# Down projection of a Trainium2 encoder layer: engine order fixed by the source, weight sums by accumulating DMA

## The chip, the cores and the metric

The kernel runs on one core of a Trainium2 chip. The metric is device time in microseconds; several runs are taken and their median counts. One further execution is recorded by the hardware profiler, and its trace is what the profile and the timelines are read from.

The engines go by short names: PE is TensorE (matmuls), DVE VectorE, ACT ScalarE, POOL GpSimd, SP SyncE. Each engine works through its own list of instructions in order; semaphores hold an instruction back until what it needs is there. SP and POOL issue DMAs here.

## The reference, cut to what matters

One encoder layer on a 256 x 2048 input in float32: a half-step feed-forward, a mixer (gated recurrence and windowed attention), and a second half-step feed-forward. The change touches both feed-forwards:

```python
def swiglu(x, w_gate_up, w_down):          # w_gate_up 2048 x 11264, w_down 5632 x 2048
    gate, up = jnp.split(x @ w_gate_up, 2, axis=-1)
    return (jax.nn.silu(gate) * up) @ w_down

ff = swiglu(rms_norm(x, pre_norm_ffn1[layer]), w_ffn1_gate_up[layer], w_ffn1_down[layer])
x = x + 0.5 * rms_norm(ff, post_norm_ffn1[layer])
```

## The kernel before

**Split arithmetic.** Each float32 operand is split in two halves of lower precision: `split_act` (L175 to L177) lets ACT round a block to `h` (L176) and DVE take the remainder `l` (L177). A product of two blocks is then three matmuls: h by h, h by l, l by h (`Blocks.three`, L441). All matmuls of the feed-forwards are of this kind, 128 x 512 wide.

**Pairs.** The contraction runs over pairs of 128 rows. A weight tile `raw` (128 x 2048) holds, for one pair, four blocks of 512 columns: b11, b12 (first 128 rows), b21, b22 (second). A plain pair costs 8 block products, 24 matmuls. A mixed pair uses a scheme of seven block products (21 matmuls) on sums of blocks, on the left (activations, `sums`, split as `sp`) and on the right (weights). On the right it needs the split of b11 (`ha`, `la` in the down projection), then b11+b12 and b22+b12 (one 128 x 1024 addition on DVE, L473), b22 plus the first of these (L477), b21 plus that (L479), and the splits of three halves of the tile, which the text calls lower, upper and last. The seven products ask, in this order, for: the first block; lower; left sums and lower; upper; upper; last; last (`Blocks.products`).

**Feed-forward.** `Gated` forms gate and up in 11 groups of 512 columns, 8 pairs each, 4 of them mixed from the third group on. These groups stand under `tc.manual_schedule()`: each engine has its instructions in the order of the source. There the weight sum b11+b12, b22+b12 of a mixed pair is not formed by DVE: `prepare` (L903) splits the first block, and POOL issues a DMA with `accum_op=add` (L910) that adds the second source block onto the tile in place; `splits` (L917) then goes on with the two dependent additions (L924, L925). After each group `boundary` (L1111) folds the seven-product partial sums (p1, p5, p6, p7) into the four result banks on DVE while PE does the last pair's products bank by bank. The last group is outside: its end is written with `fold()` and left to the scheduler, and so is all of the down projection.

**Down projection.** `Pairs` (L592) goes twice over 22 pairs of activations, once for each half of the 2048 output columns; 10 pairs of each half are mixed (even numbers up to 18), the order of the pairs is in `orders`. `Blocks.work` (L554) loads a tile of 1 MB, splits it and issues the products; a scheduler decides the order on each engine. `seven` (L463) is the mixed pair with the sum on DVE. Weight tiles rotate through three buffers `raw`; the split halves through five `h` and five `l` buffers, so that the last split of a mixed pair behind a mixed pair must wait until PE has released a half of the earlier one. Eight of the activation tiles were put away in DRAM during the gate-up groups and are fetched back into eight buffers (`fetch`, L1039), once. The last two pairs of the second half are held for `finish` (L686), which has its own fixed order.

Of the kernel before, what the change touches and what calls it, by code (L numbers as in the profile page):

```python
# [37 lines left out]
def hymba_layer_kernel(  # L38
# [37 lines left out]
    def nm(s):  # L76
        uid[0] += 1
        return f"{s}_{uid[0]}"
# [323 lines left out]
    class Blocks:  # L402
# [151 lines left out]
        def work(self, upto, among=None):  # L554


            while self.pos < upto:
                u = self.order[self.pos]
                if u in self.mixed:
                    v = self.order[self.pos + 1]  # L560
                    if v not in self.mixed and self.pos + 1 < upto:
                        self.ahead = [v]
                        self.seven(u, self.begin_next)
                    else:
                        self.seven(u)
                else:
                    if self.ahead:
                        _, raw, h, l = self.ahead
                        self.ahead = None
                        hs, ls = zip((h, l), split_half(raw, 1))  # L570
                    else:
                        hs, ls = split_load(self.source(u))
                    if self.pos == self.after + 1 and not self.within:
                        for _ in self.fold():
                            pass
                    places = [(k, m, n) for k in range(2) for m in range(2) for n in range(2)]
                    if self.pos in (self.after, self.after + 1):

                        places.sort(key=lambda at: at[1:])
                    fold = self.fold() if self.within and self.pos == self.after else None  # L580
                    for i, (k, m, n) in enumerate(places):
                        if fold and k == 0:
                            next(fold)
                        if among and i == 3:
                            among()
                        self.plain(u, hs, ls, m, n, k)
                    if fold:
                        for _ in fold:
                            pass
                self.pos += 1  # L590

    class Pairs(Blocks):  # L592

# [21 lines left out]
            self.begin(self.orders[now])  # L615

        def source(self, u):
            src = self.w[u * 2 * P : (u + 1) * 2 * P, self.now * 1024 : (self.now + 1) * 1024]
            return src.rearrange("(k p) c -> p k c", p=P)

        def left_sums(self, u):
            if u in self.kept:
# [54 lines left out]

        def first_run(self):
            self.work(len(self.orders[0]))
            for m in range(2):  # L680
# [177 lines left out]
    class Gated(Blocks):  # L858
# [20 lines left out]
        def plan(self):  # L879

            self.here = {g: MIXED_IN if g > 1 else MIXED_IN[:2] for g in range(1, NG)}
            wanted = []
            for g in range(1, NG):
                for u in range(KT // 2):
                    before = PREPARED[u] if u in self.here[g] else u
                    wanted.append((g * KT // 2 + before, g, u))
            self.wanted = [at[1:] for at in sorted(wanted)]
            self.raws, self.firsts, self.split_of = {}, {}, {}
            for pool, n in ((rawp, 3), (self.room, 2)):
                for _ in range(n):  # L890
                    raw = pool.tile([P, 2048], F32, tag="raw", name=nm("raw"), bufs=n)
                    self.load_next(raw)
# [45 lines left out]
        def take(self, g, u):  # L938
# [2 lines left out]
            del self.raws[g, u]  # L941
            first = self.firsts.pop((g, u), None)
            if first:
                before_fold = g < NG - 1 and u == KT // 2 - 2
# [36 lines left out]
    def ffn(gated, w_dn, post_gain, again, gain=None, lead=None, aside=None):  # L981

        with ExitStack() as st:
# [108 lines left out]
            def some(steps, n):  # L1092
                for _ in range(n):
                    next(steps)
# [13 lines left out]
                    aside()  # L1108
            gated.plan()

            def boundary(g):  # L1111

                a, b = room_for("z"), room_for("s")
                c, (p1, p5, p6, p7) = gated.c, gated.p
# [20 lines left out]
                some(gated.splits(g + 1, 0), 2)  # L1135

            def first_pairs(g, waiting):

# [17 lines left out]
            def pair_ahead(g, u):  # L1156
# [12 lines left out]
                if u == 5 and 1 < g <= AWAY // 2 + 1:  # L1169
                    put_away(2 * g - 4)  # L1170
                    put_away(2 * g - 3)

            waiting = units(gated.c, rs2)
            some(waiting, 2)
            with tc.manual_schedule():
                gated.prepare(1, MIXED_IN[0])
                some(gated.splits(1, 0), 2)
                for g in range(1, NG):
                    first_pairs(g, waiting)
                    for u in range(2, last - 1):  # L1180
                        pair_ahead(g, u)
                    if g < NG - 1:
                        ahead = gated.splits(g, last)
                        some(ahead, 2)
                        gated.prepare(g + 1, MIXED_IN[0])
                        for one in gated.take(g, last - 1):
                            one()
                        boundary(g)
                        waiting = units(gated.c, rest)
                        some(waiting, 2)  # L1190
            some(gated.splits(NG - 1, last), 2)
            gated.take(NG - 1, last - 1)
            a, b = room_for("z"), room_for("s")
            wide = work.tile([P, 2, 512], F32, tag="sp", name=nm("y"), bufs=3)
            gated.folded = lambda: [[a, b], [wide[:, i, :] for i in range(2)]]
            fold = gated.fold()
            final = gated.take(NG - 1, last)
            for m in range(2):
                for n in range(2):
                    next(fold)  # L1200
                    for k in range(2):
                        final[4 * k + 2 * m + n]()
            for _ in fold:
                pass
            waiting = units(gated.c, rest)
            some(waiting, 4)
            room_cm.__exit__(None, None, None)
            close_far()
            back_cm = tc.tile_pool(name=nm("hb"), bufs=AWAY, reuse_waits="tile")
            back = back_cm.__enter__()  # L1210
# [5 lines left out]
            for u in MIXED[8:]:  # L1216
                sums[u] = None
            rows = Pairs(w_dn, orders, hts, sums, work, post_gain, keep=MIXED[8:], near=MIXED[:2])
            rows.half_gain(far["pool"])
# [5 lines left out]
            for u, at in zip(MIXED[8:], (8, 12)):  # L1225
                rows.work(at)
                sums[u] = sums_again(u)
            rows.first_run()
            rows.work(NU - 4)
            back_cm.__exit__(None, None, None)  # L1230
            early_cm.__exit__(None, None, None)
            post = st.enter_context(post_pool())
# [628 lines left out]
```

## Time and profile before

| | |
|---|---|
| median of 3 runs | 1833.16 us (1830.88 to 1833.8) |
| the profiled execution, its own time | 1832.88 us |
| its span, first to last instruction | 1831.1 us |
| mean granted TensorE clock | 0.997 |
| PE busy | 1814.2 us (99%) |
| DVE busy | 1627.3 us (89%) |
| ACT busy | 1129.4 us (62%) |
| POOL busy | 114.4 us (6%) |
| DMA, mean over the span | 231 GB/s |

A row of the windows view gives a stretch in microseconds from the span's start, its length, then for PE, PE's weight loads, DVE, ACT and POOL the busy time with the count of instructions, then the granted clock as a share of full speed, the busy share of the 16 DMA engines, and GB/s. A row of the timeline gives start, duration, engine, line of the kernel, operation, what it writes and reads, and how often it stands there in a row; in square brackets how long the engine had been idle before it and what ended that. Matmuls are pipelined: one shows 0.39 us, but the next starts 0.23 us after it, so starts are compared. A row of groups gives the count, the busy time in us and the mean in ns of one, then the idle time before them.

### The profile page before, as it was taken

The page shows a single profiled execution, that of the slowest core. Times are in us where ns is not written, and L with a number is a line of the kernel's source. Part 1 is how long each engine was busy: PE and PEld are TensorE (multiplying, and loading weights), DVE is VectorE, ACT ScalarE, POOL GpSimd, SP SyncE. Part 2 cuts the span into 40 slices and gives each one's busy share as a digit, 9 for nine tenths or more (in the row PEclk, how much of TensorE's full clock was granted, in tenths as well). Part 3 has the DMA queues.
Part 4 walks back from the last instruction along what each step waited for, and adds up shares of the span by engine and source line. Part 5 has one row for each costly group of instructions (what it writes and reads, how often), then busy time and mean ns, then how long its engine had stood idle before and what let it go on. Part 6 is the DMA issues. An engine that isn't in the chain of part 4 may idle for free.

```text
span 1831.1 us, 23305 instructions
## 1 busy us (share of the span) xinstructions
PE 1814.2 (99%) x8438; PEld 1504.0 (82%) x8438; DVE 1627.3 (89%) x2071; ACT 1129.4 (62%) x1492; POOL 114.4 (6%) x115
## 2 busy tenths in 40 slices
PE   9999999999999999999999999999999999999998
PEld 6888888888887888888888888788888888888886
DVE  7999999999999998477787798899999999999897
ACT  7565666665655666476587556556666666565563
POOL 1011111111000000000000000001111111000000
PEclk9999999999999999999999999999999999999999
DMA  8789999998665566555454456789998998855565
GB/s 301 230 234 283 278 280 253 251 266 241 249 226 197 195 253 216 203 175 178 165 173 150 161 208 249 223 243 267 280 277 267 252 251 251 268 218 207 193 231 185
DMA packets 200020, 422.42 MB, mean 231 GB/s; under 512 B 10984, under 2 KB 45888, under 8 KB 199136
## 3 DMA queue, kind: packets, MB, share of 16 engines
q1 hardware_dynamic: 178880, 380.95, 59.6%
q0 software_dynamic: 21024, 39.99, 12.7%
q8 instruction: 66, 1.08, 0.2%
q14 instruction: 50, 0.41, 0.1%
HBM read 408.29 MB, written 12.60 MB: 230 GB/s over the span
## 4 chain that ended last, share of the span: by engine, by line
PE 87%; DVE 5%; ACT 3%; DMA 3%; issue 2%; POOL 0%; SPq 0%; DVEq 0%; ACTq 0%; POOLq 0%
PE pa L441 37%; PE pb L441 33%; PE pa L309 5%; DVE l L177 3%; PE pa L314 3%; DMA raw<-in_w_ffn_gate_up_dram 2%; PE pa L364 2%; PE pa L362 2%; PE pa L363 2%; ACT h L176 1%; PE pa L1074 1%; PE pb L1074 1%; PE pb L1582 0%; PE pb L1556 0%; PE pb L1660 0%
## 5 line engine op out<-in xcount | busy, mean ns | idle before, releaser
L176 ACT CAST h<-raw 128x1024 fp32r<-128x1024 f32 (+1 forms) x861 | 846.9, 1013 | 448.6 <-PE pb L441 131.9
L177 DVE TENSOR_TENSOR l<-raw,h 128x1024 fp32r<-128x1024 f32 (+1 forms) x861 | 983.1, 1171 | 118.3 <-ACT h L176 83.8
L441 PE MATMUL pa<-h,xt 128*128 128x512 f32 x1104 | 387.2, 392 | 0.1
L441 PE MATMUL pb<-h,xt 128*128 128x512 f32 x952 | 339.7, 391 | 0.4 <-DVE pb L1126 0.4
L441 PEld LDWEIGHTS pa<-h,xt 128*128 128x128 f32 x1104 | 207.2, 188 | 43.9 <-DVE xt L232 0.6
L441 PE MATMUL pa<-l,xt 128*128 128x512 f32 x552 | 215.7, 391 | 0.2 <-DVE l L177 0.2
L441 PEld LDWEIGHTS pb<-h,xt 128*128 128x128 f32 x952 | 178.6, 188 | 43.2 <-DVE pb L1133 3.5
L441 PE MATMUL pb<-l,xt 128*128 128x512 f32 x476 | 185.6, 390 | 0.0
L441 PE MATMUL pb<-h,ht 128*128 128x512 f32 x464 | 163.8, 390 | 0.0
L441 PE MATMUL pa<-h,ht 128*128 128x512 f32 x464 | 163.7, 391 | 0.0
L910 POOL DMA_DIRECT2D raw<-in_w_ffn_gate_up_dram x76 | 92.0, 1211 | 737.0 <-DVE l L177 638.8
L309 PE MATMUL pa<-xt,h 128*128 128x512 f32 x512 | 124.5, 393 | 0.2 <-ACT h L176 0.2
L441 PEld LDWEIGHTS pa<-l,xt 128*128 128x128 f32 x552 | 103.7, 188 | 21.4 <-DVE l L177 1.4
L309 PEld LDWEIGHTS pa<-xt,h 128*128 128x128 f32 x512 | 93.8, 188 | 18.6 <-ACT h L176 0.6
L441 PE MATMUL pa<-h,xs 128*128 128x512 f32 x304 | 108.5, 389 | 0.0
L441 PE MATMUL pb<-h,xs 128*128 128x512 f32 x304 | 105.9, 389 | 0.0
L441 PEld LDWEIGHTS pb<-l,xt 128*128 128x128 f32 x476 | 89.4, 188 | 17.2
L441 PEld LDWEIGHTS pa<-h,ht 128*128 128x128 f32 x464 | 87.7, 189 | 18.4
L441 PEld LDWEIGHTS pb<-h,ht 128*128 128x128 f32 x464 | 87.3, 188 | 18.1
L441 PE MATMUL pa<-l,ht 128*128 128x512 f32 x232 | 90.9, 392 | 0.0
L441 PE MATMUL pb<-l,ht 128*128 128x512 f32 x232 | 90.5, 390 | 0.0
L314 PE MATMUL pa<-xt,l 128*128 128x256 f32 x512 | 69.1, 285 | 0.0
(289 smaller groups left out, 2516.9 us busy)
## 6 DMA issues: line engine op xcount, KB each, us to landing
raw<-in_w_ffn_gate_up_dram SPq DMA_DIRECT2D x350, 512.0 KB, 6.1
raw<-in_w_ffn_down_dram SPq DMA_DIRECT2D x88, 1024.0 KB, 5.3
raw<-in_w_mix_in_dram SPq DMA_DIRECT2D x52, 1024.0 KB, 4.9
raw<-in_w_ffn_gate_up_dram POOLq DMA_DIRECT2D x76, 512.0 KB, 8.8
raw<-in_w_mix_out_dram SPq DMA_DIRECT2D x16, 1024.0 KB, 5.0
away<-ht SPq DMA_DIRECT2D x16, 512.0 KB, 6.9
ht<-away SPq DMA_DIRECT2D x16, 512.0 KB, 7.8
pg<-in_post_norm_ffn_dram SPq DMA_DIRECT2D x4, 512.0 KB, 6.7
```

The source lines that it names most:

```text
L176: nc.scalar.copy(hi, src)
L177: nc.vector.tensor_tensor(lo, src, hi.bitcast(F32), ALU.subtract)
L309: nc.tensor.matmul(slot[f], weights(hs, kk, f), xcol(xt, k), start=(k == 0), stop=(k == KT - 1))
L314: nc.tensor.matmul(slot[f][:, 0:T], weights(ls, kk, f), xcol(xt, kh * 8 + kk, 0), start=False, stop=False,)
L362: nc.tensor.matmul(dst, xh, h[:, o : o + n], start=(k == 0), stop=False)
L363: nc.tensor.matmul(dst, xh, l[:, o : o + n], start=False, stop=False)
L364: nc.tensor.matmul(dst, xl, h[:, o : o + n], start=False, stop=(k == KT - 1))
L441: nc.tensor.matmul(self.bank(at), lhs, rhs, start=(n == 1), stop=n in (ends, self.of[at]), skip_group_check=n > ends,)
L910: nc.gpsimd.dma_start(raw[:, 0:1024].rearrange("p (k c) -> p k c", k=2), self.source(u, g)[:, :, 1], accum_op=ALU.add,)
L1074: nc.tensor.transpose(bank[:, o : o + P], zs[m][:, k * P : (k + 1) * P], ident)
```

## The change

From the last gate-up group to the third last pair of the down projection's second half, everything now stands under the manual schedule, with the order of all engines written in the source:

- The last gate-up group ends with the same `boundary` as the others; the place of the next group's first pair in it is taken by the first pair of the down projection.
- Tiles of the down projection are requested in a list `coming`: when a split has released a tile, `load_down` at once requests the next of the list into it. Five tiles are in use: the three lasting ones, and two in the room of the pool `back`, whose activation buffers go from eight to four; four of the eight activation tiles are therefore fetched a second time (`fetch_at`, steps 26 to 30).
- For 15 of the 20 mixed pairs (`added`: seven in the first half, eight in the second) `prepare` splits the first block three steps ahead, and POOL issues the accumulating DMA in place of DVE's 128 x 1024 sum. Pairs 8, 10 and 18 of the first half and 10 and 18 of the second keep the sum on DVE.
- The left sums of the next mixed pair are split right behind its last weight split (`left_sums_ahead`).
- The orders of the pairs in both halves are new.

The number of matmuls is the same. DVE has 30 instructions fewer (15 in each feed-forward), POOL issues 30 DMAs more, SP 8.

```diff
@@ Gated @@
-                self.rest = 6 if g < NG - 1 else 0
+                self.rest = 6
...
                 self.raws[g, u] = raw
+            elif any(raw is one for one in self.lasting):
+                self.next_stage(raw)
@@ ffn @@
+            orders = [
+                [9, 11, 8, 13, 10, 15, 12, 1, 0, 3, 14, 5, 16, 17, 2, 7, 4, 19, 6, 18, 20, 21],
+                [7, 2, 9, 4, 11, 6, 13, 8, 10, 15, 0, 5, 12, 3, 14, 1, 16, 18, 17, 19, 20, 21],
+            ]
+            added = {0: (12, 0, 14, 16, 2, 4, 6), 1: (2, 4, 6, 8, 0, 12, 14, 16)}
+            in_order = sorted(
+                (i - 2.5 if u in added[r] else i, i) for i, (r, u) in enumerate(steps)
+            )
+            coming = [i for _, i in in_order]
...
+            def prepare(i):
+                if i < len(steps) and steps[i][1] in added[steps[i][0]]:
+                    r, u = steps[i]
+                    first_block(i)
+                    nc.gpsimd.dma_start(
+                        raws[i][:, 0:1024].rearrange("p (k c) -> p k c", k=2),
+                        Pairs.part(w_dn, u, r)[:, :, 512:1024],
+                        accum_op=ALU.add,
+                    )
+
+            def splits(i):
...
+                if i not in firsts:
+                    first_block(i)
+                    nc.vector.tensor_tensor(
+                        four[:, 0:2], four[:, 0::3], four[:, 1:2].to_broadcast([P, 2, 512]), ALU.add
+                    )
+                parts.append(split_half(raw, 1))
+                nc.vector.tensor_tensor(b22, b11, b22, ALU.add)
+                nc.vector.tensor_tensor(b21, b22, b21, ALU.add)
+                yield
+                parts.append(split_half(raw, 0))
+                yield
+                parts.append(split_half(raw, 1))
+                load_down(raw)
+                rows.left_sums_ahead(u)
+                yield
...
-            fold = gated.fold()
-            final = gated.take(NG - 1, last)
-            for m in range(2):
-                for n in range(2):
-                    next(fold)
-                    for k in range(2):
-                        final[4 * k + 2 * m + n]()
-            back_cm = tc.tile_pool(name=nm("hb"), bufs=AWAY, reuse_waits="tile")
-            orders = [
-                [9, 11, 8, 13, 10, 15, 12, 1, 14, 3, 0, 5, 2, 7, 4, 6, 17, 16, 19, 18, 20, 21],
-                [1, 0, 3, 2, 5, 4, 7, 6, 9, 8, 11, 10, 12, 13, 14, 15, 16, 18, 17, 19, 20, 21],
-            ]
-            rows.work(1)
-            rows.work(2, lambda: some(waiting, 2))
-            for i, u in enumerate((1, 3, 0, 5, 2, 7, 4, 6)):
-                fetch(u)
-                rows.work(3 + i // 2)
...
-            rows.first_run()
-            rows.work(NU - 4)
+                    boundary(g, gated.splits(g + 1, 0) if g < NG - 1 else splits(0))
+                    waiting = units(gated.c, rest)
+                    some(waiting, 2)
+                back_cm = tc.tile_pool(name=nm("hb"), bufs=AWAY // 2, reuse_waits="tile")
+                fetch_at = {2: (1, 0), 3: (3,), 5: (5,), 9: (2,), 10: (7,), 11: (4,), 13: (6,)}
+                fetch_at.update({26: (0, 5), 28: (3,), 30: (1,)})
...
+                products(0)
+                for _ in range(2):
+                    load_down(back.tile([P, 2048], F32, tag="raw", name=nm("raw"), bufs=2))
+                some(waiting, 1)
+                ahead = splits(2)
+                some(ahead, 2)
+                some(waiting, 1)
+                some(ahead, 1)
+                products(1)
+                for i in range(2, len(steps)):
...
+                    ahead = splits(i + 1)
+                    next(ahead, None)
+                    prepare(i + 3)
+                    for u in fetch_at.get(i, ()):
+                        fetch(u)
+                    next(ahead, None)
+                    products(i)
+                    for _ in ahead:
+                        pass
```

More of the change, by code (lines that the diff above doesn't have):

```diff
@@ L572, in work, with play @@
                         hs, ls = split_load(self.source(u))
[L573 to L582, printed above, removed]
-                            next(fold)
[L584 to L589, printed above, removed]
-                self.pos += 1
+                    self.play(u, hs, ls, among)
+                self.pos += 1
+        def play(self, u, hs, ls, among=None):
+            if self.pos == self.after + 1 and not self.within:
+                for _ in self.fold():
+                    pass
+            places = [(k, m, n) for k in range(2) for m in range(2) for n in range(2)]
+            if self.pos in (self.after, self.after + 1):
+                places.sort(key=lambda at: at[1:])
+            fold = self.fold() if self.within and self.pos == self.after else None
+            for i, (k, m, n) in enumerate(places):
+                if fold and k == 0:
+                    next(fold)
+                if among and i == 3:
+                    among()
+                self.plain(u, hs, ls, m, n, k)
+            if fold:
+                for _ in fold:
+                    pass
     class Pairs(Blocks):
@@ L1109, in ffn, with boundary @@
             gated.plan()
-            def boundary(g):
+            def boundary(g, ahead):
                 a, b = room_for("z"), room_for("s")
@@ new lines, in ffn, with load_down @@
+            coming = [i for _, i in in_order]
+            raws, firsts, got = {}, {}, {}
+            rows = None
+            def load_down(raw):
+                if coming and (coming[0] < NU + 17 or any(raw is one for one in gated.lasting)):
+                    i = coming.pop(0)
+                    r, u = steps[i]
+                    dst = raw.rearrange("p (k c) -> p k c", k=2)
+                    nc.sync.dma_start(dst, Pairs.part(w_dn, u, r))
+                    raws[i] = raw
+            gated.next_stage = load_down
@@ new lines, in blocks, with first_block @@
+            def blocks(raw):
+                return [raw[:, k * 512 : (k + 1) * 512] for k in range(4)]
+            def first_block(i):
+                firsts[i] = tuple(rows.one_block())
+                split_act(*firsts[i], blocks(raws[i])[0])
+            def prepare(i):
+                if i < len(steps) and steps[i][1] in added[steps[i][0]]:
+                    r, u = steps[i]
+                    first_block(i)
[4 more added lines that the diff above has]
+                    )
@@ L1173, in ffn, with products @@
+            def products(i, among=None):
+                r, u = steps[i]
+                rows.pos = i - r * NU
+                del raws[i]
+                if u in MIXED:
+                    rows.products(u, firsts.pop(i), *got.pop(i))
+                else:
+                    rows.play(u, *zip(*got.pop(i)), among)
+                rows.pos += 1
             waiting = units(gated.c, rs2)
@@ L1181, in ffn @@
                         pair_ahead(g, u)
+                    some(gated.splits(g, last), 2)
                     if g < NG - 1:
-                        ahead = gated.splits(g, last)
-                        some(ahead, 2)
                         gated.prepare(g + 1, MIXED_IN[0])
[L1186 to L1190, printed above, removed]
@@ L1228, in ffn @@
-            rows.first_run()
-            rows.work(NU - 4)
-            back_cm.__exit__(None, None, None)
-            early_cm.__exit__(None, None, None)
-            post = st.enter_context(post_pool())
+                    for one in gated.take(g, last - 1):
+                        one()
+                    boundary(g, gated.splits(g + 1, 0) if g < NG - 1 else splits(0))
+                    waiting = units(gated.c, rest)
+                    some(waiting, 2)
+                room_cm.__exit__(None, None, None)
@@ new lines, in ffn @@
+                close_far()
+                back_cm = tc.tile_pool(name=nm("hb"), bufs=AWAY // 2, reuse_waits="tile")
+                back = back_cm.__enter__()
+                fetch_at = {2: (1, 0), 3: (3,), 5: (5,), 9: (2,), 10: (7,), 11: (4,), 13: (6,)}
+                fetch_at.update({26: (0, 5), 28: (3,), 30: (1,)})
+                again_at = {8: 16, 14: 18}
+                for u in MIXED[8:]:
+                    sums[u] = None
+                rows = Pairs(w_dn, orders, hts, sums, work, post_gain, keep=MIXED[8:], near=MIXED[:2])
@@ new lines, in ffn @@
+                some(waiting, 2)
+                ahead = splits(1)
+                some(ahead, 2)
+                products(0)
[3 more added lines that the diff above has]
+                ahead = splits(2)
+                some(ahead, 2)
+                some(waiting, 1)
+                some(ahead, 1)
+                products(1)
+                for i in range(2, len(steps)):
+                    if i == NU + 18:
+                        back_cm.__exit__(None, None, None)
+                        early_cm.__exit__(None, None, None)
+                        post = rows.post = st.enter_context(post_pool())
+                    ahead = splits(i + 1)
[6 more added lines that the diff above has]
+                    for _ in ahead:
+                        pass
+                    if i in again_at:
+                        sums[again_at[i]] = sums_again(again_at[i])
+                    if i == 8:
+                        rows.half_gain(far["pool"])
+                    if i == NU - 1:
+                        rows.second_run()
```

54 lines of the change are left out of this document (31 added, 23 removed).

## The prediction

> **What bounds the kernel now.** I read the page first: engine times and the chain that ended last.
>
> ```profile
> PE 1814.2 (99%) x8438; PEld 1504.0 (82%) x8438; DVE 1627.3 (89%) x2071; ACT 1129.4 (62%) x1492; POOL 114.4 (6%) x115
> PE 87%; DVE 5%; ACT 3%; DMA 3%; issue 2%; POOL 0%; SPq 0%; DVEq 0%; ACTq 0%; POOLq 0%
> ```
>
> TensorE (PE) is the bound. The change leaves every matmul in place, so it can only remove moments when PE has none. The windows of 25 us tell where those are: the stretches of the two down projections (about 477 to 703 and 1594 to 1814 us) are full except for these.
>
> ```profile
> 525.00:550.00 25.00, 25.00 (x112) 20.71 (x111) 24.66 (x31) 13.46 (x15) 0.00 (x0) 1.00 0.65 245
> 550.00:575.00 25.00, 22.96 (x94) 18.27 (x93) 23.70 (x27) 14.56 (x17) 0.00 (x0) 0.93 0.52 188
> 1675.00:1700.00 25.00, 24.24 (x107) 19.82 (x107) 23.41 (x25) 15.61 (x17) 0.00 (x0) 1.00 0.64 243
> ```
>
> The second columns are PE: 94 matmuls instead of 112 in one window, 107 in the other, while DVE is 94 to 99% busy. The timeline of PE shows how. 549.91 and 554.67 are the starts of two seven-product pairs in a row (4, then 6).
>
> ```profile
> 549.91 0.39 PE L441 MATMUL pa<-ha,ht 128*128 128x512 f32 x1
> 554.67 0.39 PE L441 MATMUL pa<-ha,ht 128*128 128x512 f32 x1
> 557.85 0.39 PE L441 MATMUL pb<-h,sp 128*128 128x512 f32 x1
> 559.51 0.49 PE L441 MATMUL pb<-h,sp 128*128 128x512 f32 x1 [1.27 <-ACT h L176]
> 560.77 0.50 PE L441 MATMUL pb<-l,sp 128*128 128x512 f32 x1 [0.77 <-DVE l L177]
> 561.34 0.39 PE L441 MATMUL pb<-h,ht 128*128 128x512 f32 x1
> 565.44 0.39 PE L441 MATMUL pb<-h,ht 128*128 128x512 f32 x1
> ...
> 1674.68 0.65 PE L441 MATMUL pb<-h,sp 128*128 128x512 f32 x2
> 1676.08 0.50 PE L441 MATMUL pb<-l,sp 128*128 128x512 f32 x1 [0.76 <-DVE l L177]
> 1676.64 0.39 PE L441 MATMUL pb<-h,ht 128*128 128x512 f32 x1
> ```
>
> One pair is 21 products in 4.76 us, 0.227 each; a plain pair of 24 is 5.44. From 557.85 to 561.34 four products took 3.49 instead of 0.91: **2.6 us** lost. From 561.34 to 565.44 eleven took 4.10 instead of 2.49, at the lowered clock (0.93 in the window): **1.6 us** more. The same place of the second feed-forward loses 1.96 - 0.91 = **1.05 us** and no clock.
>
> The Trainium skill ("TensorE: Matmul & The Clock Gate", section "What's actually happening") lets the clock fall to half after an idle window of about 3.4 us. By that rule waits of 1.27 and 0.77 us would not do it, the 1.6 us would have another cause and could stay, and the sum below would end at 1830.2. The rows set the slow products right behind the wait, and they decide; one chance in twenty, inside the second rival.
>
> What was late? The timeline of DVE at that place:
>
> ```profile
> 557.63 0.68 DVE L479 TENSOR_TENSOR raw<-raw 128x512 f32<-128x512 f32 x1
> 558.24 0.68 DVE L177 TENSOR_TENSOR la<-raw,ha 128x512 fp32r<-128x512 f32 x1
> 558.84 0.68 DVE L177 TENSOR_TENSOR sp<-sums,sp 128x512 fp32r<-128x512 f32 x1
> 559.49 2.36 DVE L177 TENSOR_TENSOR l<-raw,h 128x1024 fp32r<-128x1024 f32 x2
> ```
>
> PE wants the last split of pair 6 (the l of 559.49), and DVE does it behind two operations that belong to the pair after it (la, sp). So DVE is late by its total load over two mixed pairs, and the scheduler's order adds to it. Start to start, a 512-wide operation costs DVE 0.60 and a 1024-wide one 1.14 us (2.36 less the last one's own 1.22).
>
> **The change part by part.** Removed: the 1024-wide weight sum on DVE (L473) in 15 of 20 mixed pairs of each feed-forward.
>
> ```profile
> L473 DVE TENSOR_TENSOR raw<-raw 128x1024 f32<-128x1024 f32 x20 | 24.4, 1220 | 0.2
> ```
>
> 15 x 1.14 = 17 us of DVE per feed-forward, beside PE, worth nothing by itself. A mixed pair falls from 0.60 + 1.14 + 1.2 + 3 x 1.14 + 0.60 = 7.0 us to 5.8, against 4.76 of PE; mixed plus plain from 9.2 to 8.1 against 10.2. The new lists leave mixed pairs adjacent at 6, 18 and (second half) 8, 10 and 16, 18; the first of each has its sum by DMA. With 4, 6 both on DVE gone, I remove all of the three losses, and a smaller one of 0.3 at the end:
>
> ```profile
> 1798.40 0.61 PE L441 MATMUL pb<-h,sp 128*128 128x512 f32 x2
> 1799.05 0.50 PE L441 MATMUL pb<-l,sp 128*128 128x512 f32 x1
> 1799.39 0.40 PE L441 MATMUL pb<-h,sp 128*128 128x512 f32 x1
> ```
>
> (three products in 0.99 instead of 0.68). Sum removed: 2.6 + 1.6 + 1.05 + 0.3 = **5.5 us**.
>
> Added and moved: the last gate-up group now folds as the others do, and the down projection starts under a fixed order. What that order does is seen at a boundary between groups now:
>
> ```profile
> 220.60 0.39 PE L441 MATMUL pa<-h,xt 128*128 128x512 f32 x1
> 226.15 0.39 PE L441 MATMUL pa<-h,xt 128*128 128x512 f32 x1
> 232.38 0.48 PE L441 MATMUL pa<-h,xt 128*128 128x512 f32 x1
> ```
> ```profile
> 224.51 2.35 DVE L177 TENSOR_TENSOR l<-raw,h 128x1024 fp32r<-128x1024 f32 x2
> 226.78 0.74 DVE L1054 SCALAR_TENSOR_TENSOR z<-pa,scales,z 128x512 f32<-128x512 f32 x1
> ...
> 254.11 0.69 DVE L924 TENSOR_TENSOR raw<-raw 128x512 f32<-128x512 f32 x1
> ...
> 255.45 5.37 DVE L177 TENSOR_TENSOR l<-raw,h 128x1024 fp32r<-128x1024 f32 x5
> ```
>
> The 24 products that close a group take 5.55 instead of 5.44: +0.1 in each feed-forward, **0.2**. Then the ledger of DVE, on this boundary's clock: the first down pair is split by 226.78; two gate products 0.66 each, 228.1; second pair 2 x 1.14, 230.4; then pair 8, which keeps its sum on DVE: 0.60 + 1.14 + 1.14, two dependent adds 1.34 (254.11 to 255.45), 1.14, two transposed activations 1.2, 1.14, the split of its left sums 0.60, together 8.3: 238.7. PE: down starts at 226.15, transposes end at 232.38, pair 8 begins 5.44 later at 237.8 and asks for its left sums six products on, at 239.2. Slack 0.5 us. In order, every wait of ACT or DVE ahead of that split (transposes, a load) delays what is behind it. I enter **1.0 us** for both feed-forwards of such new waits (bounds 0 and 1.05 at each of some four tight places, 4.2: FFN2's stall is the nearest row). SP: the two extra raw tiles are requested only after the first pair's products, but a released tile is refilled four pairs ahead from then on, 20 us against a landing of 5.3; the four second fetches (0.5 MB) have that lead as well. Cost 0, behind PE; without that cover a load would show at 5.3. POOL has nothing else queued while it waits for the split of a first block. The gain vector's load moves from the start to pair 9 and is read only at the end of the half: 0.
>
> ```profile
> raw<-in_w_ffn_down_dram SPq DMA_DIRECT2D x88, 1024.0 KB, 5.3
> q1 hardware_dynamic: 178880, 380.95, 59.6%
> q0 software_dynamic: 21024, 39.99, 12.7%
> 203.00:244.00 41.00, 41.00 (x186) 33.84 (x185) 39.02 (x47) 25.52 (x30) 4.84 (x4) 1.00 0.93 273
> ```
>
> DMA: 59.6% of 1831 over 381 MB is 2.87 us per MB on SP's queue, 5.8 on the accumulating one. A first half now moves 27.8 MB and accumulates 3.7: 80 + 21 = 101 us of its 113. A gate-up group runs at 0.93, with four accumulations, DVE at 39.0 of 41 us, and PE without a gap. That row is why I take the fixed order as able to hold PE.
>
> Sum, on the profiled execution: 1832.88 (span 1831.1) - 5.5 + 0.2 + 1.0 = **1828.6 us**. That execution stands 0.3 under the median, 1833.16 (1830.88 to 1833.8).
>
> **The rivals.** **A new chain through the accumulating DMA (slower).** In the new order DVE splits the first block of pair i+2 right behind the two adds of pair i, and those adds wait for pair i's accumulation. So from mixed pair to mixed pair runs a loop: split, POOL, landing, two adds, split.
>
> ```profile
> 243.84 0.69 DVE L177 TENSOR_TENSOR l<-raw,h 128x512 fp32r<-128x512 f32 x1
> 244.94 1.20 POOL L910 DMA_DIRECT2D raw<-in_w_ffn_gate_up_dram  x1 [11.67 <-DVE l L177]
> DMA to landing us min/median/max: 5.6/8.8/10.7
> ...
> DMA to landing us min/median/max: 6.6/6.6/6.6
> ...
> DMA to landing us min/median/max: 9.0/9.0/9.0
> ```
>
> The first landing row is of all 76 accumulations, the next two of those issued at 203.14 and 244.94, which stand alone as the new ones would (no other accumulation in flight). 244.53 to 244.94 is 0.41; adds and split are 1.34 + 0.69; so a turn is 2.44 us plus the landing, against 10.2 us of PE for a plain and a mixed pair. It decides from a landing of 7.8. At 6.6 it hides. At 9.0 each of the six links of the first half (12, 0, 14, 16, 2, 4, 6) is 1.2 late, less 1.7 that the ledger above, carried on to pair 12, has in hand: 5.5 us, 11 in both: 1838.6. Behind the waiting add stand all of DVE's later splits, and behind those PE. Against it: of twelve such single issues nine landed in 6.5 to 6.8, like that of 203.14, the others in 8.0, 8.7 and 9.0. For it: the fetches and the 1 MB loads of the first half share those microseconds.
>
> The Trainium skill ("DMA: Bandwidth & Descriptors", section "Anatomy of one DMA") gives 2.0 us + bytes / 436e3. By that an accumulation of 512 KB lands in 3.2 us, the loop is never seen, and this rival has no chance. The trace says 5.6 at the least, so it keeps one.
>
> **The stall only moves.** The left-over sums at 10 and 18 still cost 7 us or more of DVE against 4.76. If DVE is as late there as it is at 1676 now, four times 1.05 come back: 1831.8; the change would not do what it says.
>
> **How the numbers follow.** Forecast 52% (1827.6 to 1829.5), moved stalls or the clock 33% (1829 to 1834), chain 15% (1834 to 1842). A measurement of this kernel can tell about 0.2%, 3.7 us, from no change. Faster than 1829.5: the forecast and 2 of the second, 54%. Within: 31 + 2 = 33%. Slower: 13%. The range leaves out most of the chain and a gain beyond every loss named: 1826.9 to 1835.0.
>
> **What would show it.** Right: windows with 112 matmuls and clock 1.00 at the old places, DVE idle by 10 us more per down projection, no wait of PE on a split there over 0.5 us. The ledger is wrong if PE waits in the first mixed pair (8); the chain holds if DVE idles before the adds on the software queue, with landings over 7.8, and PE gaps recur every 10 us. The forecast as a whole is wrong if the two old stalls stay, or if the half clock comes without them.

## The result, and the profile after

| | before | after |
|---|---|---|
| median (6 runs each) | 1832.35 us | 1848.94 us (1848.07 to 1854.68) |
| ratio of the means, 95% interval | 1 | 1.0096 (1.0083 to 1.011) |
| span of the profiled execution | 1831.1 us | 1846.4 us |

The changed kernel is slower by 16.6 us; 1828.6 was forecast, and the range ended at 1835.0. The engine times and the chain of the page of after:

```profile
PE 1819.5 (99%) x8438; PEld 1504.8 (82%) x8438; DVE 1601.5 (87%) x2041; ACT 1128.7 (61%) x1492; POOL 150.7 (8%) x145
PE 71%; DMA 9%; issue 9%; DVE 8%; ACT 3%; POOL 1%; SPq 0%; DVEq 0%; ACTq 0%; POOLq 0%
```

DVE has the 30 instructions fewer that the change names and is busy 26 us less, and the share of PE in the last chain falls from 87 to 71%, with DMA up from 3 to 9. Windows of the changed kernel:

```profile
500.00:525.00 25.00, 22.96 (x100) 18.37 (x100) 19.44 (x22) 13.28 (x16) 2.42 (x2) 1.00 0.88 257
525.00:550.00 25.00, 25.00 (x112) 20.73 (x111) 19.88 (x25) 13.88 (x16) 2.44 (x2) 1.00 1.04 348
550.00:575.00 25.00, 24.16 (x106) 19.59 (x106) 23.16 (x29) 15.78 (x18) 2.41 (x2) 1.00 0.84 268
625.00:650.00 25.00, 22.13 (x89) 17.23 (x88) 20.64 (x23) 13.13 (x17) 2.44 (x2) 0.93 0.78 254
675.00:700.00 25.00, 23.47 (x105) 19.13 (x104) 22.62 (x25) 15.90 (x17) 0.00 (x0) 1.00 0.86 324
1675.00:1700.00 25.00, 25.00 (x111) 20.43 (x110) 23.02 (x29) 14.73 (x17) 2.17 (x2) 1.00 0.88 286
1750.00:1775.00 25.00, 23.16 (x94) 18.39 (x93) 21.26 (x24) 14.22 (x17) 2.41 (x2) 0.93 0.84 282
```

At the pairs 4 and 6 PE no longer waits in either feed-forward, and 1675 to 1700 is full: what was to be removed is removed. But PE now has holes elsewhere, and in the largest, 500 to 525 and 625 to 650, DVE is *not* busy: 19.4 and 20.6 of 25 us. Before, a hole stood where DVE was 94 to 99% busy; now DVE itself is waiting. The views of waits, of PE and then of DVE (us in total, times, longest), say for what:

```profile
PE pa L441 <- DVE sp L177: 6.7, 9, 1.1
PE pa L441 <- ACT sp L176: 3.3, 3, 1.5
PE pa L441 <- DVE pa L535: 2.6, 2, 1.5
```
```profile
DVE raw L1259 <- DMA raw<-in_w_ffn_down_dram: 30.8, 19, 4.9
```

PE waits for the left sums (`sp`) and for the fold (L535), 12.6 us in all; DVE stands 30.8 us ahead of the first dependent addition (L1259), until an accumulation has landed, that is, until its data are in place. One such place, timelines of PE, DVE and POOL:

```profile
510.92 0.39 PE L441 MATMUL pa<-h,ht 128*128 128x512 f32 x1
512.28 0.50 PE L441 MATMUL pa<-h,sp 128*128 128x512 f32 x1 [0.97 <-ACT sp L176]
512.62 0.40 PE L441 MATMUL pa<-l,sp 128*128 128x512 f32 x1
514.09 0.73 PE L441 MATMUL pa<-h,sp 128*128 128x512 f32 x2 [1.07 <-DVE sp L177]
```
```profile
502.97 1.23 DVE L177 TENSOR_TENSOR l<-raw,h 128x1024 fp32r<-128x1024 f32 x1
509.14 0.69 DVE L1259 TENSOR_TENSOR raw<-raw 128x512 f32<-128x512 f32 x1 [4.94 <-DMA raw<-in_w_ffn_down_dram]
509.86 0.69 DVE L1260 TENSOR_TENSOR raw<-raw 128x512 f32<-128x512 f32 x1
510.47 0.68 DVE L177 TENSOR_TENSOR la<-raw,ha 128x512 fp32r<-128x512 f32 x1
511.08 2.35 DVE L177 TENSOR_TENSOR l<-raw,h 128x1024 fp32r<-128x1024 f32 x2
513.35 0.68 DVE L177 TENSOR_TENSOR sp<-sums,sp 128x512 fp32r<-128x512 f32 x1
```
```profile
498.17 1.22 POOL L1232 DMA_DIRECT2D raw<-in_w_ffn_down_dram  x1 [42.23 <-DVE la L177]
511.57 1.21 POOL L1232 DMA_DIRECT2D raw<-in_w_ffn_down_dram  x1 [12.18 <-DVE la L177]
```

The accumulation issued at 498.17 landed 10.88 us later. Until then DVE waited; behind its two adds stood the split of the first block of the next mixed pair, two steps on (`la`, 510.47), so the next accumulation went out only at 511.57, 13.4 us after the one before it instead of 10.2. The left sums came last of all, at 513.35 to 514.03, and PE, which wants them as its third product, stood from 511.15. This is the loop of the first rival, seen in every part. Landings, from the view of the accumulating line in after (min, median, max), the rows of DMA issues of after, and SP's timeline ahead of 498.17:

```profile
DMA to landing us min/median/max: 6.0/6.3/10.9
```
```profile
raw<-in_w_ffn_down_dram SPq DMA_DIRECT2D x88, 1024.0 KB, 7.5
raw<-in_w_ffn_down_dram POOLq DMA_DIRECT2D x30, 512.0 KB, 6.3
ht<-away SPq DMA_DIRECT2D x24, 512.0 KB, 9.4
```
```profile
490.28 0.93 SPq L1065 DMA_DIRECT2D ht<-away  x2
492.74 0.38 SPq L1216 DMA_DIRECT2D raw<-in_w_ffn_down_dram  x1
493.16 0.51 SPq L1065 DMA_DIRECT2D ht<-away  x1
```

The median is 6.3, but the landings of the first feed-forward that PE paid for (10.88, 10.23 at 540.75, 10.71 at 619.07) are far above it. All three had fetches of activation tiles (`ht`) in flight that SP issued 3 to 8 us earlier. A fourth late one (9.10 at 586.39) fell where three plain pairs stand in a row, and cost PE nothing.

### The profile page after: what moved, and what is told of

Its sections match the earlier page's. It is cut to its first block, busy times and chain, and to the rows that moved or that the text cites. A ratio compares the mean times of both kernels' runs of the same rounds, so it can differ in the third digit from the quotient of the medians.

```text
span 1846.4 us, 23441 instructions
## 1 busy us (share of the span) xinstructions
PE 1819.5 (99%) x8438; PEld 1504.8 (82%) x8438; DVE 1601.5 (87%) x2041; ACT 1128.7 (61%) x1492; POOL 150.7 (8%) x145
## 4 chain that ended last, share of the span: by engine, by line
PE 71%; DMA 9%; issue 9%; DVE 8%; ACT 3%; POOL 1%; SPq 0%; DVEq 0%; ACTq 0%; POOLq 0%
PE pa L441 29%; PE pb L441 25%; DMA raw<-in_w_ffn_down_dram 6%; PE pa L309 5%; DVE l L177 3%; PE pa L314 3%; DMA raw<-in_w_ffn_gate_up_dram 2%; PE pa L364 2%; PE pa L363 2%; PE pa L362 2%; ACT h L176 1%; DVE raw L1259 1%; DVE la L177 1%; POOL raw L1232 0%; PE pa L1098 0%
## 5 line engine op out<-in xcount | busy, mean ns | idle before, releaser
L441 PEld LDWEIGHTS pa<-l,xt 128*128 128x128 f32 x552 | 103.8, 188 | 20.6 <-DVE l L177 0.5
L441 PE MATMUL pa<-h,sp 128*128 128x512 f32 x176 | 63.8, 404 | 10.1 <-DVE sp L177 6.7
```

The costliest lines, as they stand in the source:

```text
L441: nc.tensor.matmul(self.bank(at), lhs, rhs, start=(n == 1), stop=n in (ends, self.of[at]), skip_group_check=n > ends,)
```

## The experiments

Theory A: late landings, entering through the chain. Theory B: the written order itself is at fault, whatever forms the sums. Of theory A it was open what makes a landing late (fetches, weight loads, bytes or their order), and whether a single late landing or the chain does the harm. Times are medians; ratios, of the means, are against runs of the kernel before on the same chip.

| run | time, us | ratio, 95% interval |
|---|---|---|
| e1_no_accum | 1841.99 | 1.0050 (1.0035 to 1.0065) |
| e2_left_first | 1854.91 | 1.0121 (1.0104 to 1.0138) |
| e3_no_fetch | 1832.90 | 1.0002 (0.9993 to 1.0012) |
| e4_split_ahead | 1838.18 | 1.0030 (1.0018 to 1.0042) |
| e5_fetch_pool | 1838.05 | 1.0030 (1.0020 to 1.0039) |
| e6_ahead_fold | 1835.17 | 1.0012 (1.0003 to 1.0021) |
| e7_ahead_pool | 1835.60 | 1.0013 (1.0004 to 1.0023) |
| e8_ahead_spread | 1835.32 | 1.0011 (1.0002 to 1.0021) |
| e9_ahead_fit | 1829.33 | 0.9984 (0.9975 to 0.9993) |
| e10_fit_pool | 1829.41 | 0.9987 (0.9978 to 0.9996) |
| e11_fit_no_accum | 1840.78 | 1.0047 (1.0034 to 1.0060) |
| e12_fit_left | 1828.34 | 0.9981 (0.9972 to 0.9990) |

**e1_no_accum: the sums back on DVE.**

```diff
-added = {0: (12, 0, 14, 16, 2, 4, 6), 1: (2, 4, 6, 8, 0, 12, 14, 16)}
+added = {0: (), 1: ()}
```

> The list of accumulated pairs is emptied: every order written by hand stays, all 20 sums are formed by DVE. Theory A (late landings): the changed kernel loses because an accumulation that lands 8 to 11 us after its issue instead of 6 holds DVE before the two dependent adds, and the split of the left sums stands behind them. Without accumulations those waits are gone; what stays is the wait at the fold (1.7 + 1.2 us) and DVE's load at the three adjacent pairs of each half-and-half (7.0 us each against 4.76, 1 to 2.6 us at a place): 1834 to 1841. Theory B (the written order itself, whatever forms the sum, puts the left sums too late): 1845 or more.

1842.0, just above what theory A allowed and well below B's. So in this order the accumulations cost 7 us more than the DVE work that they replace, but the order with all sums on DVE is itself 10 us slower than the kernel before. The list also decides which tiles are requested early, so that order goes with it. With no accumulation left, PE waits behind DVE's own work: of the 7.5 us below, 5.8 lie at adjacent mixed pairs (6 then 18, 8 then 10), the rest in pair 4 of each half.

```profile
PE pa L441 <- DVE sp L177: 4.2, 8, 0.6
PE pa L441 <- ACT sp L176: 3.3, 4, 1.1
```

**e2_left_first: the left sums ahead of the adds.**

```diff
                 parts.append(split_half(raw, 1))
+                rows.left_sums_ahead(u)
                 nc.vector.tensor_tensor(b22, b11, b22, ALU.add)
...
                 load_down(raw)
-                rows.left_sums_ahead(u)
```

> Only the split of the left sums is moved: ahead of the two adds instead of behind the last weight split. The accumulations land as before (8 to 11 us at the late places). If what PE waits for is that split held up behind the waiting adds, it now waits for the next thing, the upper half, which is due 0.68 us later in the pair and is split 1.7 us earlier after the landing: 2.4 us of room at each place. Most waits (0.5 to 1.9 us) go, a rest of 1 to 2 us stays at the pair 8 then 10 of the second half, and the fold's 2.9: 1836 to 1841. If the late landing hits PE whatever stands behind it: 1845 to 1849.

1854.9: a miss on both sides, 6 us slower than the changed kernel. No wait for `sp` is left, but PE waits for the last things behind the adds instead, above all for the fold:

```profile
PE pa L441 <- DVE pa L535: 10.6, 4, 4.0
PE pa L441 <- DVE l L177: 6.8, 7, 2.0
```

So moving one split chose who waits. That its own 0.6 us ahead of the adds are paid by all that follows is argued; ahead of the longest fold wait ACT also stands 2.10 and 1.23 us for plain loads.

**e3_no_fetch: no activation tile is fetched.**

```diff
                     for u in fetch_at.get(i, ()):
-                        fetch(u)
+                        hts[u] = hts[9]
```

> Leaves out the 12 fetches of activation tiles of each feed-forward (6 MB); the pairs 0 to 7 use another pair's activations, so part of the result is not computed. Tells what makes landings late. If the fetches crowd the accumulations: the landings of 10.9, 10.2, 10.7 us beside them fall to 6.0 to 6.5, and the waits that followed (2.4, 1.0 and 4.8 us in the first feed-forward, some 5 in the second) go: 1834 to 1840. If it is the 1 MB weight loads: landings of 8 to 11 stay, 1844 to 1849.

1832.9, a little under the range and all of the 16 us gone, though the chain and every order stand as in the changed kernel. PE's and DVE's waits, and the accumulations:

```profile
PE pa L441 <- DVE pa L535: 2.2, 2, 1.1
...
PE pa L441 <- DVE sp L177: 0.8, 1, 0.8
```
```profile
DVE raw L1259 <- DMA raw<-in_w_ffn_down_dram: 7.6, 10, 1.9
```
```profile
DMA to landing us min/median/max: 5.9/6.3/9.1
```

The landings that had been 10.88, 10.23 and 10.71 are 6.33, 6.20 and 6.17. The fourth, behind weight loads alone, stays at 9.12 (9.10 in after), and again costs nothing.

**e4_split_ahead: the chain cut.**

```diff
-                    next(ahead, None)
                     prepare(i + 3)
+                    next(ahead, None)
```

> The split of the first block three steps ahead, and with it the issue of its accumulation, moves ahead of the two adds that wait for the accumulation of the pair before. That breaks the chain from landing to landing: each accumulation is issued 1.3 us sooner plus whatever the adds waited (up to 4.9). Chain theory: what stays is a single late landing at a time, issued 2 us sooner: 1836 to 1842. If the waits come from single late landings and not from the chain: 1844 to 1848. If the weight tile of the pair three steps on has not landed so early, DVE waits for it instead: 1850 or more.

1838.2, 10.7 us less. The fetches are where they were, and landings are now *longer*; line of the accumulations and waits of DVE in e4_split_ahead:

```profile
DMA to landing us min/median/max: 5.9/8.6/11.9
```
```profile
DVE raw L1259 <- DMA raw<-in_w_ffn_down_dram: 5.7, 5, 1.9
```

A median of 8.6 costs less than one of 6.3, because the accumulation is issued sooner (the first link's at 493.72 instead of 498.17) and no longer waits for the one before. The two come with the same edit and were not separated. So it takes late landings and this order together to do the harm; taking away either gives back 11 to 16 us.

**e5_fetch_pool: same bytes, other order.**

```diff
-                nc.sync.dma_start(hts[u].bitcast(F32)..., away[u])
+                nc.gpsimd.dma_start(hts[u].bitcast(F32)..., away[u])
```

> As the changed kernel, with one edit: the 12 fetches of activation tiles go out on POOL's queue, behind the accumulation of the same step, instead of SP's. The bytes are the same. If an accumulation is late because transfers issued just before it have to drain first, it is now ahead of the fetches of its own step: landings mostly 6 to 7 us, and the time falls to 1834 to 1840. If it is late because the same bytes share the engines in those microseconds, the landings stay at 8 to 11: 1843 to 1849. Against both: a fetch waits for a buffer that PE must release, and an accumulation behind it on POOL waits too: above 1850.

1838.05, with the chain in place (the ten runs reach from 1834.99, the profiled one, to 1842.68). The accumulations, now ahead of the fetches of their step, land so:

```profile
DMA to landing us min/median/max: 6.0/6.4/9.9
```

The bytes are the same, so it is largely what stands ahead of an accumulation that makes it late. The edit changes the queue of the fetches along with their place, and these two were not separated. The one of 9.9 went out at 538.45 while a fetch that POOL had issued at 529.87 was in flight, until 541.2.

**e6_ahead_fold, e7_ahead_pool, e8_ahead_spread: what is left of e4.** All three have e4's edit and the following in the fold; e7 adds the fetches on POOL, e8 moves fetches by a step.

```diff
-            if self.rooms == 4:
+            soon = isinstance(self, Pairs)
+            if self.rooms == 4 and not soon:
                 second_row()
                 last()
             yield
             add(c[0][0], c[0][0], y11, ALU.add)
+            if self.rooms == 4 and soon:
+                second_row()
+                last()
@@ e8 @@
-                fetch_at = {2: (1, 0), 3: (3,), 5: (5,), 9: (2,), 10: (7,), 11: (4,), 13: (6,)}
-                fetch_at.update({26: (0, 5), 28: (3,), 30: (1,)})
+                fetch_at = {2: (1, 0), 4: (3,), 6: (5,), 10: (2, 7), 12: (4,), 14: (6,)}
+                fetch_at.update({25: (0,), 27: (5,), 28: (3,), 30: (1,)})
```

> The first block's split ahead of the adds (e4_split_ahead, 1838.2), and in the fold at the end of a half the addition that PE waits for (c00) stands second instead of fourth on DVE. e4 still waits 1.4 - 0.23 us at the fold of each second half. If those waits come from the fold's own order on DVE they go: 1838.2 - 2.3 = 1835.9. If the fold waits for the split of a held pair's weight tile and thus for its load: 1838.

> e6_ahead_fold with the fetches on POOL's queue. Its largest wait left is at pair 8 then 10 of the second half (3.4 - 0.7 us and half clock behind it, some 4 in the first feed-forward, 3 in the second), where the accumulation landed in 11.9 us beside two fetches. If the queue order makes it late: that landing falls to 6 to 8 us, and the time to 1829 to 1833. If the bytes do: 1835 to 1837.

> e6_ahead_fold with the fetches on SP's queue still, but each moved by a step, so that it is issued in a step without an accumulation (0 and 5 of the second half in steps 25 and 27 instead of both in 26). The accumulation of pair 8 in the second half then has no fetch in flight: 6 to 8 us instead of 11.9, and its wait of some 4 and 3 us goes: 1829 to 1833. If a fetch a step earlier holds the weight loads behind it on SP (it waits for a buffer), a load is late instead: 1838 or more.

1835.2, 1835.6, 1835.3. The fold's own order was worth some 3.0 us (2.3 expected): the intervals of e4 and e6 overlap, but the two fold waits of 1.0 us that e4 still had are gone in e6's trace. The fetches, once the chain is cut, are worth nothing, against what I expected: the wait at pair 8 then 10 keeps its size whether the landing is 8.97 (e7) or 11.13 (e8). Its cause is seen in e8_ahead_spread, timelines of ACT and DVE:

```profile
628.50 0.62 ACT L176 CAST ha<-raw 128x512 fp32r<-128x512 f32 x1 [2.81 <-PE pa L441]
```
```profile
629.16 0.69 DVE L177 TENSOR_TENSOR la<-raw,ha 128x512 fp32r<-128x512 f32 x1 [2.05 <-ACT ha L176]
629.89 1.22 DVE L1258 TENSOR_TENSOR raw<-raw 128x1024 f32<-128x1024 f32 x1
```

The moved split wants a third `ha` buffer where there are two. ACT stands until PE gives one up, DVE stands behind ACT, and behind that stands the sum of pair 10, which PE needs first. Cutting the chain everywhere had made a new wait at one place.

**e9_ahead_fit, e10_fit_pool, e11_fit_no_accum, e12_fit_left: the version that holds.** e9 is e8, e10 is e7, each with this; e11 is e9 with e1's edit, e12 is e9 with e2's.

```diff
-                    prepare(i + 3)
+                    sum_here = i + 1 < len(steps) and steps[i + 1][1] in MIXED and i + 1 not in firsts
+                    if not sum_here:
+                        prepare(i + 3)
                     next(ahead, None)
+                    if sum_here:
+                        prepare(i + 3)
```

> e8_ahead_spread, except that where the next pair forms its sum on DVE the split of the first block three steps ahead stays behind that pair's adds. In e6, e7 and e8 the one wait left (1.9 and 1.0 us at pair 8 then 10 of each second half) has the same size whatever the landing (8.97 or 11.1 us), and DVE stands 2.05 us there behind an ha that ACT can't write until PE gives up one of the two ha buffers. If the buffer is the cause: the wait shrinks to the 0.3 to 0.5 us that e5 has there, 2 us less in each feed-forward: 1835.3 - 4 = 1831.3, just under the kernel before. If DVE's own load at two adjacent pairs is: 1835.

> The same with the fetches on POOL's queue in their old steps instead of SP's in other steps (e7_ahead_pool with the first block's split kept behind the adds of pair 10). If only the chain and the order among transfers matter, it does as e9: 1831.3. If an accumulation is held on POOL behind a fetch that waits for its buffer: 1834 or more.

> e9_ahead_fit with the list of accumulated pairs emptied: all 20 sums on DVE in the same written order, so what the accumulation itself is worth once it is not late. e1_no_accum gave 1842.0; the fold's earlier addition takes off its 0.4 + 0.4, the moved fetches nothing: 1841. So e9 less this one, some 10 us, would be the gain of DVE's removed sums in this order. If the sums on DVE cost nothing when nothing is late: within 2 us of e9.

> e9_ahead_fit with the left sums split ahead of the adds, as in e2_left_first. There it cost 6 us, because the adds and all splits behind them came 0.6 us later on DVE and the waits moved to the last weight split and to the fold (4.3 and 1.8 us). With landings no longer late, those have room: the last waits for sp (0.3 to 0.5 us at three places) go and it is 0.5 to 1.5 us faster than e9. If the loss in e2 was due to the place itself: 3 to 6 us slower than e9.

e9 and e10 give 1829.3 and 1829.4, 6 us under e8 and e7 (I had expected 4) and faster than the kernel before by 2.8 us. Windows of both down projections in the kernel before, then in e9_ahead_fit:

```profile
477.00:703.00 226.00, 223.96 (x984) 184.40 (x983) 214.06 (x241) 133.46 (x158) 0.00 (x0) 0.99 0.62 228
1594.00:1814.00 220.00, 219.21 (x968) 180.28 (x967) 209.56 (x237) 129.73 (x152) 0.00 (x0) 1.00 0.59 218
```
```profile
477.00:703.00 226.00, 225.87 (x1001) 186.69 (x1000) 204.90 (x231) 138.66 (x165) 18.74 (x16) 1.00 0.87 286
1594.00:1814.00 220.00, 219.87 (x975) 181.82 (x974) 196.12 (x220) 130.06 (x154) 18.13 (x15) 1.00 0.84 275
```

PE is busy 225.87 of 226 us, with DVE 9 us lighter and the DMA engines at 0.87 instead of 0.62. e11, with the sums back on DVE, is 11.5 us slower than e9: as soon as nobody waits for them, the accumulations are worth that in this order, though they still land in 8.6 us at the median and 11.1 at the most. e12 gives 1828.3: the left sums' place, harmful in e2, does no harm once landings have room; its 1 us under e9 is not separated from it by the intervals.

## Why the prediction was wrong

- **Removed, 5.5 us: right for the stalls.** Those of pairs 4, 6 are gone in after (pair 18 behind 6 waits 0.48 and 0.25 us), and e9 and e12 come out 2.8 and 3.8 us under the kernel before. Both carry further edits: 1828.6 is about what this order gives when nobody waits for an accumulation or the fold, not what the change gave.
- **Boundary, +0.2: right in kind.** The 24 products that close the last group take 5.46 and 5.50 us in after (first and second feed-forward) instead of 5.44: 0.1 together.
- **Ledger of the first mixed pair (8): right.** PE's first wait is at 511, in pair 12, the third.
- **New waits, 1.0 us (bounds 0 to 4.2): the term that failed in size.** PE's waits for `sp` and the fold are 12.6 us, and two stretches of half clock come on top (some 1.6 us each: eight products 0.43 us apart instead of 0.23). It was sized from the old stall of DVE's load; most of these waits stand behind a DMA.
- **"SP: cost 0": the step that failed.** I asked whether a load would be late for its user. No wait of PE ends on one, though a weight load's landing rose from 5.3 to 7.5 us and ACT stood 0.25 to 1.51 us for each of four loads just ahead of the folds. I did not ask what SP's transfers do to the accumulations that go out among them. e3 prices that at all of the 16 us, and e5 gives back 10.9 of them with the same bytes.
- **The first rival was the mechanism, and I gave it 15%.** Its point of decision, 7.8 us, holds only roughly: the landings of 7.54 and 7.89 in the first feed-forward were followed by no wait of PE, the four over 10 in both (10.88, 10.23, 10.71, 10.05) all were; of the five around 9 one was (9.04 at 1732.77). The 7.42 behind that one (1744.33), issued late in its turn, was followed by waits too, at pair 10. The chance came from twelve issues in the gate-up groups that landed alone, nine in 6.5 to 6.8; no fetch was in flight there, and I wrote down that the fetches share the microseconds without pricing it. Its price, 1838.6, fell 10 us short because it counted six links of the first half at 9.0: the landings were up to 10.9, DVE does the left sums last, the second half is hit as well (638 to 645 and 1761 to 1768, with the half clock), and the fold pays too.
- **The fold was on nobody's list.** In the order of the source, c00's addition stands behind four others of the fold; the scheduler had it behind two. 2.6 us in after; e6 gives back 3.0.
- **"The stall only moves": in part.** With DVE's sum at 10 behind the accumulated 8, one product stands 0.51 us after the one before it, instead of 0.23, even in e9 (634.03 to 634.54), and e1 and e11 show what the same order costs without accumulations.
- **The fixed order is able to hold PE: true of e9, false of after.** In the gate-up row three of the four accumulations are issued ahead of the adds of another pair; the down projection's order puts nearly each behind the adds of the one before. That this is what keeps the gate-up groups free of waits was not tried.

## What to carry to other kernels

When DVE work is handed to a DMA in a fixed order, write down the loop from one such DMA to the next (what must be done before it can be issued, and what that stands behind), and price its landing among the transfers of *that* stage, not of a quieter one. Issue it before anything that waits for the DMA ahead of it; then check the buffers, since an operation moved forward takes one sooner. A written order also freezes details that a scheduler had got right (here the fold's first addition), so compare the order of both versions at every place where another engine waits.

## What the runs showed of the hardware

**A landing depends on what is still in flight at its issue.** Of the 30 accumulations of 0.5 MB in after, 13 went out when the last of SP's earlier transfers had at most 2.3 us to go: they took 6.0 to 6.3 us. The four over 10 us had 6.2 to 7.6 us of such transfers ahead of them. That is not all: the landings of 9.10 and 9.18 (586.39, 1708.81) had some 3 us ahead, and a load that SP issued 0.7 to 0.8 us behind them. The Trainium skill ("DMA: Bandwidth & Descriptors", section "Anatomy of one DMA") gives 2.0 us + bytes / 436e3, an estimate of 3.2 us. The shortest in the down projection, in any run here, is 5.8.

**The half clock is decided in windows of 3.41 us, and half a window of idle PE is enough.** The granted clock in after is 0.50 from 642.27 to 645.68 and from 1765.25 to 1768.66, each time for 3.41 us, and the two starts lie 1122.98 us apart, 329 times 3.413. Windows of after, laid at that spacing:

```profile
509.15:512.56 3.41, 2.44 (x11) 1.74 (x10) 3.38 (x5) 2.94 (x4) 0.99 (x1) 1.00 0.49 201
512.56:515.98 3.42, 2.35 (x10) 1.61 (x10) 3.42 (x4) 2.87 (x4) 0.22 (x1) 1.00 0.65 113
638.86:642.27 3.41, 0.84 (x3) 0.30 (x2) 3.41 (x5) 3.39 (x4) 1.22 (x1) 1.00 0.16 13
642.27:645.68 3.41, 3.38 (x8) 2.71 (x9) 3.38 (x3) 1.63 (x3) 0.00 (x0) 0.50 1.04 198
1761.84:1765.25 3.41, 1.72 (x6) 1.16 (x7) 3.41 (x4) 2.86 (x5) 1.11 (x1) 1.00 0.42 53
1765.25:1768.66 3.41, 3.41 (x9) 2.65 (x9) 2.87 (x4) 1.67 (x3) 0.00 (x0) 0.50 1.07 284
```

Waits of 0.97 and 1.07 us at 512 to 514 fall into two windows, PE is busy 2.44 and 2.35 us of them, and the clock stays. Waits of 0.78 and 1.07 us at 1762 to 1764, less in sum, fall into one, PE is busy 1.72 us of it, and the next window runs at half clock. So the sum of the waits alone does not tell. In the down projections of all traces the same spacing fits: no window with PE idle up to 1.67 us (e2_left_first, from 639.55) was followed by half clock, and each with 1.69 us or more was. The half clock in before (561.62 to 565.03) follows a window with 2.04 us, so its 1.6 us did belong to the waits. One window outside them with 1.56 us was too (e4_split_ahead, from 1179.51), and the profile's ends of matmuls are modelled, so about half a window is as near as the limit is known. The Trainium skill ("TensorE: Matmul & The Clock Gate", section "What's actually happening") asks for an idle window of about 3.4 us. The trace of after agrees with the length and not with the idleness: PE was idle for 50 and 75% of the two windows that brought the half clock. The same waits, of 1.5 and 0.6 us at pair 10, fell into one window in e6_ahead_fold (633.16 to 636.57) and brought it, and were parted by a window's end in e8_ahead_spread (at 635.51) and did not.
